# Moving the sample's score steps of the gated-linear-attention layer from the end of a block into the stretches of the next one

## The chip, the cores and the metric

The kernel runs on one core of one Trainium2 chip. The metric is the time of one execution on the device in microseconds (us). The engines in the profile are TensorE (PE, with its weight loads apart as PEld), VectorE (DVE), ScalarE (ACT), GpSimd (POOL) and SyncE (SP, here the issuer of most DMAs).

## The reference

One inference step of a decoder with two layers runs on a prompt of 2048 positions and on a sample group of 8 sequences with 4 new tokens each, 32 rows. The first layer is gated linear attention with 4 heads (128 key and 512 value elements each). Cut to what matters:

```
proj = rmsnorm(h) @ w_in                       # q, k, v, gate, g_low
log_a = log_sigmoid(g_low @ w_gate2 + b_gate) / 16
# in chunks, for each head:
b = cumsum(log_a)
rel = where(causal, b[t] - b[s], -inf)
scores = einsum('td,sd,tsd->ts', q, k, exp(rel))
out = (q * exp(b)) @ state + scores @ v
state = exp(b_last) * state + (k * exp(b_last - b)).T @ v
# then
o = rmsnorm(out) * silu(gate); h = h + o @ w_out
```

The prompt starts from a zero state; each of the 8 sequences starts from a state of its own (`state_gla`, 128 x 512 for each sequence and head), which is read, used and written back. The second layer is windowed attention on keys and values that are projected once; the change does not touch it.

## The kernel before

**Tiles.** The first layer works head by head, h = 0 to 3, and for each head in 4 blocks of 512 positions, (h, j), each of 4 chunks of 128. A product of two f32 operands is made of three matmuls on f16 halves (`PASSES`): an operand is split by ScalarE (L194 or L197, the high half) and VectorE (L195 or L198, the low half). Of each block the q and k projections (`qk_steps`, evicted by ScalarE at L430 into qT and kT), the decay (`decay_steps`, L366 to L372) and the prompt's scores (`level_steps`: a diagonal and 7 levels of halving spans, tiles E and X, PSUM bank lev) are prepared one block ahead. For each chunk, `vg_steps` projects V (split into v at L197/L198) and the gate (ScalarE at L477, VectorE at L478, tile sg), and `chunk_steps` makes the readout o and the state update kv. All projections use the PSUM tag pj with two banks; lev and kv have one bank each.

**The sample.** After the last block of a head, `SampleA` projects the 32 rows and returns 14 steps (L690 to L820): `diag`, two `level` steps, `mid`, `stack`, eight times `seq` and `fin`. `diag` computes the decay of the 32 rows and the diagonal of their scores S; a `level` makes an exponential (L721 to L725), splits it into the tile ssm (L194/L195), multiplies it on TensorE into lev, and writes the result into S under a mask (L731). `mid` makes the f16 copy Sh of S and the masked queries; `stack` transposes keys and values; `seq` reads one sequence's state (loaded for two sequences at a time, L785), splits it into pst (L197/L198), multiplies, updates it (L795, L796) and stores the pair (L800). The state tiles come from a ring (tag W) in which the third pair takes the buffer of the first. `fin` is at L806 to L814.

**The order.** The program is written as steps; `weave` puts a list of steps evenly between the steps of another, `mix` merges two lists. A block starts with `weave(cur.vg_steps(0, ...), prev_tail)`, where `prev_tail` is what the block before left over: its last chunk and the decay of the next block. Then come the q and k projections of the next block, and three stretches c = 0, 1, 2, in each of which V and gate of chunk c + 1 are woven with chunk c, some of the next block's levels, a share of the sample's steps (`sparts`), and preparations of weights for the second layer (L197/L198 from wraw, L248). In the first block of a head (j = 0, h > 0) the gate of chunk 0 comes after the q and k projections. The framework's scheduler then orders each engine's instructions by priorities that follow this text and by when it takes operands to be ready; the order on TensorE is fixed by the text only in the second layer. Each engine works through its instructions in order.

The last head's sample has no next block, and all its steps go into `prev_tail`. So the steps stand in three places where there is a next block: (1,0), (2,0) and (3,0).

Of the kernel before, what the change touches and what calls it, by code (L numbers as in the profile page):

```python
# [9 lines left out]
F32 = mybir.dt.float32  # L10
# [21 lines left out]
SMP = NS * TS  # L32
# [42 lines left out]
def _body(tc, nc, cp, sb, ps, dr, i, o):  # L75
    uniq = [0]

    def nm(s):
        uniq[0] += 1
        return f"{s}_{uniq[0]}"  # L80

    def T(tag, shape, dt, bufs=None):
        return sb.tile(shape, dt, tag=tag, name=nm(tag), **({} if bufs is None else {"bufs": bufs}))
# [67 lines left out]
    def weave(main, fill):  # L151

        main, fill = list(main), list(fill)
        done = 0
        for n, f in enumerate(main):
            f()
            upto = len(fill) * (n + 1) // len(main)
            for g in fill[done:upto]:
                g()
            done = upto  # L160
        for g in fill[done:]:
            g()
# [5 lines left out]
    def mix(a, b):  # L168

        out = []  # L170
        weave([lambda f=f: out.append(f) for f in a], [lambda f=f: out.append(f) for f in b])
        return out
# [125 lines left out]
    def norm_T(xh, n, dst, both=False, flat=False):  # L298
# [4 lines left out]
        if both:  # L303
            junk = T("S", [P, 512], F32, 1)
            dve.tensor_tensor_reduce(junk, xh[1], xh[1], 1.0, 0.0, ALU.mult, ALU.add, ss[:, 1:2])
# [110 lines left out]
    class Blk:  # L416
# [67 lines left out]
        def level_steps(self):  # L484


            def diag():
                S = self.S = T("S", [P, 512], F32, 1)
                Sv = S.rearrange("p (c t) -> p c t", t=P)
                E = T("E", [P, 512], F32, 2)  # L490
# [9 lines left out]
            def level(li, m):  # L500
                bt, S, qT, kT = self.bt, self.S, self.q, self.k
                NB = 256 // m
# [19 lines left out]
                for c in range(4):  # L522
# [8 lines left out]
                dve.copy_predicated(  # L531
                    S.rearrange("p (B z m) -> p B z m", z=2, m=m)[:, :, 1, :],
                    lvm[:, li, :].rearrange("p (B m) -> p B m", m=m),
# [135 lines left out]
    class SampleA:  # L669
# [18 lines left out]
        def steps(self):  # L688
# [4 lines left out]
            bx = {}  # L693
# [5 lines left out]
            def diag():  # L699
                if h == 0:  # L700
                    ogTs[0] = T("ogTs", [P, 16, 2, SMP], F16, 1)
                bx["bt"] = T("sbt", [P, SMP], F32, 1)
                logs(gls, h, SMP, rms, bx["bt"])
                qs, ks = self.qkv[:, 0, :], self.qkv[:, 1, :]
                S = bx["S"] = T("S", [96, SMP], F32, 1)
                X0 = dup3(T("ssm", [P, 2, 3, SMP], F16, 1), ks)
                X1 = dup3(T("sq2", [P, 2, 3, SMP], F16, 1), qs)
                pd = PT("lev", [P, 512])
                for n, (a, b) in enumerate(PASSES):
                    mm(pd[:96, :SMP], f(X0, a), X1[:, b, 0, :], start=n == 0, stop=n == 2)  # L710
                dve.tensor_tensor(S, pd[:96, :SMP], id3, ALU.mult)
# [194 lines left out]
    cur = Blk(0, 0, hw[0])  # L906
# [31 lines left out]
    prev_tail = []  # L938
    samp = None
    sparts = []  # L940

    for n, (h, j) in enumerate(blocks):
        nxt = None
        if n + 1 < len(blocks):
            h2, j2 = blocks[n + 1]
            nxt = Blk(h2, j2, hw[h2])
        side = []
        if n == 0:
            side = u_steps(2)
        elif n == 1:  # L950
            side = u_steps(3) + [us_step]
        lv = nxt.level_steps() if nxt else []
        last = j == NBL - 1
        late = j == 0 and h > 0
        if n > 0:
            weave(cur.vg_steps(0, (0,) if late else (0, 1)), prev_tail)
        if last:
            samp = SampleA(h, cur.w)
            for f in samp.proj_steps():
                f()  # L960
        if nxt:
            for f in nxt.qk_steps():
                f()
        if late:
            weave(cur.vg_steps(0, (1,)), [])
        if last:
            ch = [cur.chunk_steps(c) for c in range(3)]
            weave([f for c in range(1, 4) for f in cur.vg_steps(c, (0,))], ch[0] + lv[:3] + ch[1][:3] + lv[3:5] + ch[2][:3])
            run(hw[h + 1].v.steps() if h + 1 < AH else wo.steps()[4:])
            for c in range(1, 4):  # L970
                weave(cur.vg_steps(c, (1,)), (ch[c - 1][3:] if c > 1 else []) + lv[3 + c * 2 : 5 + c * 2])
            for f in ch[2][3:]:
                f()
            run(hw[h + 1].g.steps() if h + 1 < AH else wo1.steps()[8:])
        else:
            for c in range(3):
                if n == len(blocks) - 2:
                    if c == 0:
                        wo_aside()
                    more = (wo1.steps()[:8] + wo.steps()[:4])[c * 4 : c * 4 + 4]  # L980
                else:
                    more = side[c * 2 : c * 2 + 2] if n < 2 else some(PR[j])
                weave(cur.vg_steps(c + 1, (0, 1) if n else (1,)), mix(cur.chunk_steps(c) + lv[(0,3,6)[c]:(3,6,8)[c]], sparts[(0,3,7)[c]:(3,7,99)[c]]) + more)
                if j == NBL - 2 and h + 1 < AH and c == 0:
                    hw[h + 1] = head_weights(h + 1)
                    for u in hw[h + 1].qk:
                        for f in u.steps():
                            f()
            sparts = []
        if n == 0:  # L990
            gain(gs_o, i["a_out_norm"][0], later)
            gain(gs_kv, i["kv_norm"], later)
            gain(gs_b, i["b_norm"][0], later)

            def bf_const(name, shape):
                f = T("pst", shape, F32, 2)
                later(f, i["c_" + name])
                t = C(name, shape, BF16)
                dve.tensor_copy(t, f)
                return t  # L1000

            madd = bf_const("madd", [P, 2, P])
            nsink = C("nsink", [P, NKV * GRP], F32)
            later(nsink, i["b_sinks"][0].partition_broadcast(P))
            dve.tensor_scalar(nsink, nsink, -1.0, None, ALU.mult)
            gq = C("gq", [P, 2, HD], F32)
            for x_, g in enumerate((i["b_q_norm"][0], i["k_norm"])):
                later(gq[:, x_, :], g.partition_broadcast(P))

            lvs = C("lvs", [96, 2, 16], U8)  # L1010
            f_ = T("pst", [96, 2, 16], F32, 2)
            later(f_, i["c_lvs"])
            dve.tensor_copy(lvs, f_)
            id3 = C("id3", [96, SMP], F32)
            later(id3, i["c_id3"])
            bm = C("bm", [96, NS], F32)
            later(bm, i["c_bm"])
            bmq = T("spp", [P, NS, SMP], F16, 1)
            bmf = T("pst", [P, NS, SMP], F32, 2)
            later(bmf, i["c_bmq"])  # L1020
            dve.tensor_copy(bmq, bmf)
            smask = bf_const("smask", [P, 2, 160])
            rts = C("rts", [SMP, 4, HD], F32)
            for y_ in range(2):
                for z_ in range(2):
                    x_ = 2 * y_ + z_
                    later(rts[:, x_, :], i["c_rope_s"][z_])
                    if z_ == 0:
                        dve.tensor_tensor(rts[:, x_, :], rts[:, x_, :], gq[:SMP, y_, :], ALU.mult)
                    else:  # L1030
                        H2 = HD // 2
                        dve.tensor_tensor(rts[:, x_, :H2], rts[:, x_, :H2], gq[:SMP, y_, H2:], ALU.mult)
                        dve.tensor_tensor(rts[:, x_, H2:], rts[:, x_, H2:], gq[:SMP, y_, :H2], ALU.mult)
            sel = T("sq1", [GRP, P], F32, 1)
            later(sel, i["c_sel"])
            skT = C("skT", [GRP, NKV], F32)
            later(skT, i["b_sinks"][0].rearrange("(g r) -> r g", r=GRP))
            psk = PT("tr", [P, NKV], bufs=2)
            nc.tensor.matmul(psk, sel, skT, start=True, stop=True)
            sinkr = C("sinkr", [P, NKV], F32)  # L1040
            dve.tensor_scalar(sinkr, psk, 8.0, None, ALU.mult)
        prev_tail = cur.chunk_steps(3) + (nxt.decay_steps() if nxt else [])
        if j == NBL - 1:
            sparts = samp.steps()
            prev_tail += sparts[:4]
            del sparts[:4]
            if nxt is None:
                prev_tail += sparts
        cur = nxt
# [631 lines left out]
    for t in range(-3, NKV * NCH):  # L1681
        fill = []
        n = t + 3
        if n < NKV * NCH:
            g, c = divmod(n, NCH)
# [55 lines left out]
    for p_ in range(NCH // 2):  # L1741
        more = []
        if p_ + 1 < NCH // 2:
            nxt = pairs[p_ + 1]
            ld, sm = [lambda x=x, nxt=nxt: nxt.load(x) for x in (2, 3, 0, 1)], nxt.sums()
            more = ld[:2] + sm[:2] + ld[2:3] + sm[2:6]
# [3 lines left out]
        if p_ in (3, 4):  # L1750
            n = p_ - 3
# [88 lines left out]
```

## Time and profile before

| | |
|---|---|
| runs | 2853.12, 2844.96, 2841.90 us (median 2844.96) |
| profiled execution | 2844.21 us, span 2842.2 us, mean clock 0.987 |
| TensorE busy | 2723.1 us (96%) |
| VectorE busy | 1843.3 us (65%) |
| ScalarE busy | 1441.8 us (51%) |
| GpSimd busy | 1066.3 us (38%) |
| block (1,0), (2,0), (3,0): starts at about | 359, 632, 907 us |

A row of a timeline gives the start and length in us, the engine, the line, the operation, its output and inputs, their shapes, how many in a row (x), and in brackets the idle time before with what ended it. A row of the waits gives the engine and the tile that waited, the instruction that ended the wait, the sum in us, the number of waits and the longest. A row of the windows gives the stretch, its length, an engine's busy time, and the clock that TensorE was granted (1.00 is full speed).

### The profile page before, as it was taken

To read this page: it belongs to the slowest core of one execution; us is meant where nothing else is said; L and a number is where in the kernel's file an instruction comes from. 1 tells how busy PE (TensorE), PEld (TensorE's weight loads), DVE (VectorE), ACT (ScalarE), POOL (GpSimd) and SP (SyncE) were. 2 spreads that over 40 slices of the span, in tenths; PEclk is the share of its full clock that TensorE was granted. 3 is DMA by queue.
4 is the path that set the end of the run, shared out by engine and by line. 5 is a ranking of instruction groups with operands and counts; after the bars stand their busy time and mean duration, and the time that the engine had idled before them with its cause. 6 is when DMAs were issued, how large, how long until landed. Compare 5 with 4: busy or idle time off the path is not lost.

```text
span 2842.2 us, 51647 instructions
## 1 busy us (share of the span) xinstructions
PE 2723.1 (96%) x19070; PEld 1389.7 (49%) x19070; DVE 1843.3 (65%) x3815; ACT 1441.8 (51%) x3385; POOL 1066.3 (38%) x1471
## 2 busy tenths in 40 slices
PE   6899999999999999999899999999999999988999
PEld 4444444444454444445344555555555555553444
DVE  5767787668767785435512665677767767777653
ACT  6655666466546654433312555566666666651110
POOL 1242223222322221115504686666657657530000
PEclk9999999999999999999999999999999999999999
DMA  8351325123412442799977677957866788797651
GB/s 211 90 126 36 101 89 163 34 86 123 131 38 82 149 111 74 183 229 293 240 169 182 117 145 129 217 116 131 178 124 130 145 164 175 150 216 168 138 120 57
DMA packets 795606, 395.04 MB, mean 139 GB/s; under 512 B 647504, under 2 KB 721176, under 8 KB 795320
## 3 DMA queue, kind: packets, MB, share of 16 engines
q1 hardware_dynamic: 782392, 356.01, 55.4%
q0 software_dynamic: 10880, 35.66, 3.4%
q8 instruction: 149, 2.44, 0.4%
q14 instruction: 105, 0.86, 0.1%
q10 hardware_dynamic: 2080, 0.07, 0.0%
HBM read 144.28 MB, written 107.54 MB: 89 GB/s over the span
## 4 chain that ended last, share of the span: by engine, by line
PE 59%; DVE 12%; DMA 9%; ACT 8%; issue 6%; POOL 4%; SPq 1%; ACTq 0%; DVEq 0%; POOLq 0%
PE pj L101 34%; PE o L101 11%; PE tr L101 9%; PE kv L101 3%; ACT o L1278 2%; PE lev L101 2%; DVE v L198 2%; DMA pre<-pst 2%; ACT v L197 1%; DVE o L1273 1%; DMA wraw<-in_a_w_in_dram 1%; DVE W L198 1%; POOL ogT L195 1%; DVE lev L1273 1%; DVE X L195 1%
## 5 line engine op out<-in xcount | busy, mean ns | idle before, releaser
L101 PE MATMUL pj<-W,uT 128*128 128x512 f16 x5088 | 1199.7, 381 | 6.9 <-ACT qT L430 3.1
L101 PEld LDWEIGHTS <-uT 128*128 128x128 f16 x6976 | 653.3, 98 | 712.7 <-issue 35.2
L101 PE MATMUL tr<-W,uT 128*128 128x512 f16 x1536 | 365.5, 379 | 0.0
L186 POOL TENSOR_SCALAR rs_m<-ss 128x1 f32<-128x1 f32 (+3 forms) x190 | 46.0, 242 | 671.0 <-ACT og L611 230.8
L101 PEld LDWEIGHTS <-X 128*128 128x128 f16 x2744 | 184.5, 98 | 143.8 <-issue 11.7
L1278 ACT ACTIVATE o<-o,mx 128x256 f32<-128x256 f32 (+1 forms) x384 | 168.6, 439 | 163.7 <-DVE mx L1273 159.6
L101 PE MATMUL pj<-uT,W 128*128 128x512 f16 (+1 forms) x912 | 187.4, 356 | 27.6 <-DMA uT<-ogT 23.4
L1273 DVE CUSTOM_DVE_ANT_0 o<-o,madd,nsink 128x256 f32<-128x256 f32 (+1 forms) x384 | 183.9, 479 | 41.8 <-PE o L101 37.2
L187 POOL TENSOR_TENSOR rs_r<-rs_m,mhalf 128x1 f32<-128x1 f32 (+2 forms) x186 | 186.2, 1001 | 14.4
L198 DVE SCALAR_TENSOR_TENSOR v<-o,v 128x512 f16<-128x512 f32 (+1 forms) x192 | 128.8, 671 | 92.6 <-ACT v L197 90.4
L101 PEld LDWEIGHTS <-W 128*128 128x128 f16 x2448 | 129.8, 99 | 113.9 <-issue 19.7
L101 PEld LDWEIGHTS <-v 128*128 128x128 f16 x976 | 95.8, 98 | 126.7 <-issue 9.8
L508 POOL TENSOR_TENSOR E<-bt 128x256 f32<-128x256 f32 x96 | 74.2, 774 | 198.4 <-DVE X L195 118.0
L195 POOL TENSOR_TENSOR ogT<-og,ogT 128x512 f16<-128x512 f32 x68 | 87.9, 1293 | 154.8 <-ACT ogT L194 150.4
L101 PEld LDWEIGHTS <-sg 128*128 128x128 f16 x800 | 78.6, 99 | 102.6 <-DMA sg<-ogd 7.2
L101 PE MATMUL o<-gl,X 128*128 128x256 f16 (+1 forms) x768 | 113.7, 271 | 5.2 <-DMA X<-qe 2.8
L101 PE MATMUL pj<-W,v 128*128 128x512 f16 x448 | 107.0, 386 | 9.5 <-DVE st L1614 5.9
L197 ACT ACTIVATE v<-o 128x512 f16<-128x512 f32 (+1 forms) x192 | 111.2, 579 | 3.6
L1278 ACT ACTIVATE lev<-lev,mx 128x256 f32<-128x256 f32 (+1 forms) x128 | 56.5, 441 | 103.8 <-DVE mx L1273 101.8
L248 POOL DMA_DIRECT2D pre<-pst x72 | 50.5, 703 | 141.3 <-DVE pst L198 130.0
L195 DVE TENSOR_TENSOR X<-E,X 128x512 f16<-128x512 f32 x128 | 94.6, 739 | 12.8 <-ACT X L194 12.4
L194 ACT ACTIVATE X<-E 128x512 f16<-128x512 f32 x128 | 79.5, 621 | 43.4 <-PE lev L101 20.0
(468 smaller groups left out, 5021.4 us busy)
## 6 DMA issues: line engine op xcount, KB each, us to landing
pre<-pst POOLq DMA_DIRECT2D x72, 256.0 KB, 3.5
W<-pre SPq DMA_DIRECT2D x36, 512.0 KB
ogd<-ogT SPq DMA_DIRECT2D x68, 256.0 KB
wraw<-in_a_w_in_dram SPq DMA_DIRECT2D x64, 256.0 KB
wraw<-in_b_w_in_dram SPq DMA_DIRECT2D x64, 256.0 KB
oge<-ogT SPq DMA_DIRECT2D x64, 256.0 KB
wraw<-in_a_w_out_dram SPq DMA_DIRECT2D x32, 256.0 KB
X<-in_x_prompt_dram SPq DMA_DIRECT2D x32, 256.0 KB
```

The lines of the kernel that those rows point to most:

```text
L101: return order(nc.tensor.matmul(*a, **k))
L186: pool.tensor_scalar(m[:n, :k], ss, a, b, ALU.mult, ALU.add)
L187: pool.tensor_tensor(r[:n, :k], m[:n, :k], mhalf[:n, :k], ALU.pow)
L194: act(hi, src, AF.Copy)
L195: eng.tensor_tensor(lo, src, hi, ALU.subtract)
L197: act(hi, src, AF.Copy, scale=sc)
L198: dve.scalar_tensor_tensor(lo, src, sc, hi, ALU.mult, ALU.subtract)
L248: nc.gpsimd.dma_start(self.pre[:, :, half * 512 : half * 512 + 512], t)
L508: pool.tensor_tensor(Ev[:, :, 0, :], ref, btv[:, :, 0, :], ALU.subtract)
L1273: dve.tensor_tensor_reduce(pm[:, z], pm[:, z], madd.rearrange("p a b -> p (a b)")[:, (2 - nk) * P :], -0.125, nsink[:, g * GRP + h : g * G ...
L1278: act(pm[:, z], pm[:, z], AF.Exp, scale=-1.0, bias=nm_[:, h : h + 1], accum_out=bx["sum"][:, h : h + 1])
```

## The change

Three edits. The sample's score tile gets a tag of its own (sS) in place of the prompt's (S). At the end of a head's last block only `diag` goes into the tail that runs at the next block's start; before, the two levels and `mid` went there too. The remaining 13 steps are shared over the three stretches as 4, 5 and 4 (levels, `mid`, `stack`; sequences 0 to 4; sequences 5 to 7 and `fin`) where the remaining 10 were shared as 3, 4 and 3 (`stack` and sequences 0 and 1; 2 to 5; 6, 7 and `fin`).

```diff
-                S = bx["S"] = T("S", [96, SMP], F32, 1)
+                S = bx["S"] = T("sS", [96, SMP], F32, 1)
...
-                weave(cur.vg_steps(c + 1, (0, 1) if n else (1,)), mix(cur.chunk_steps(c) + lv[(0,3,6)[c]:(3,6,8)[c]], sparts[(0,3,7)[c]:(3,7,99)[c]]) + more)
+                weave(cur.vg_steps(c + 1, (0, 1) if n else (1,)), mix(cur.chunk_steps(c) + lv[(0,3,6)[c]:(3,6,8)[c]], sparts[(0,4,9)[c]:(4,9,99)[c]]) + more)
...
             sparts = samp.steps()
-            prev_tail += sparts[:4]
-            del sparts[:4]
+            prev_tail += sparts[:1]
+            del sparts[:1]
```

TensorE at the start of block (2,0), where the next block's k projection ends (its input W_5723) and the gate projection of chunk 0 begins (W_6862); before:

```order
L101 MATMUL pj_7079<-uT_157,W_5723 128x512
L101 LDWEIGHTS uT_156
L101 MATMUL pj_7106<-W_6862,uT_156 128x512 [waits Activation_49]
L101 LDWEIGHTS uT_156
L101 MATMUL pj_7106<-W_6862,uT_156 128x512
L101 LDWEIGHTS ssm_7000 [waits Activation_49]
L101 MATMUL lev_7003<-ssm_7000 96x16 [waits DVE_49]
```

The sample's first level stands between the second and the third matmul of the gate. With the change it stands behind the whole gate projection of chunk 0 and 16 matmuls of V of chunk 1 (into pj_7090), which itself has a wait on ScalarE (`...` for rows that repeat):

```order
L101 MATMUL pj_7062<-W_6889,uT_156 128x512
L101 LDWEIGHTS uT_156
L101 MATMUL pj_7090<-W_6638,uT_156 128x512 [waits Activation_49]
...
L101 MATMUL pj_7090<-W_6656,uT_156 128x512
L101 LDWEIGHTS ssm_7123
L101 MATMUL lev_7126<-ssm_7123 96x16 [waits DVE_49]
```

ScalarE at the same place, from the decay of the block (E, L366 to L368) and the levels' exponentials (L723) to the eviction of q (qT); before:

```order
L366 ACTIVATE E_7061<-tr_7059,bgate 128x512 [waits DVE_49,Activation_49]
L723 ACT_TABLE_LOAD
L723 ACTIVATE k_1190_6994<-k_1190_6994 128x32 [waits DVE_49]
L367 ACTIVATE E_7061<-E_7061 128x512 [waits Activation_49]
L723 ACTIVATE k_1194_7011<-k_1194_7011 128x32 [waits DVE_49]
L430 ACTIVATE qT_7077<-pj_7041 128x512 [waits PE_49]
```

And with the change, where qT stands ahead of L367 and of the second level's exponential, and the table load has gone to an earlier place:

```order
L366 ACTIVATE E_7017<-tr_7015,bgate 128x512 [waits DVE_49,Activation_49]
L723 ACTIVATE k_1205_7117<-k_1205_7117 128x32 [waits DVE_49]
L430 ACTIVATE qT_7033<-pj_6997 128x512 [waits PE_49]
L367 ACTIVATE E_7017<-E_7017 128x512 [waits Activation_49]
L723 ACTIVATE k_1214_7153<-k_1214_7153 128x32 [waits DVE_49]
```

SyncE in block (1,0), where the first head's pairs of states are stored (L800) and the next are loaded (L785), among stores of finished chunks (ogd) and a load for the second layer (L894); before:

```order
L623 DMA ogd_97<-ogT_4188 256x1x512 [waits DMAHW4_49,Pool_49]
L894 DMA pst_4309<-in_c_rope_dram 128x512 [waits DMAHW5_49,DMASW5_49,PE_49]
L800 DMA out_st_s_dram<-W_4221 128x2x512 [waits DMAHW6_49,DVE_49]
L785 DMA W_4433<-in_state_gla_dram 128x2x512 [waits DMAHW7_49,DMAHW6_49]
L623 DMA ogd_98<-ogT_4398 256x1x512 [waits DMAHW0_49,Pool_49]
```

And with the change, where the store of the first pair stands behind one more store of a chunk:

```order
L623 DMA ogd_97<-ogT_4155 256x1x512 [waits DMAHW5_49,Pool_49]
L623 DMA ogd_98<-ogT_4366 256x1x512 [waits DMAHW6_49,Pool_49]
L800 DMA out_st_s_dram<-W_4313 128x2x512 [waits DMAHW7_49,DVE_49]
L785 DMA W_4491<-in_state_gla_dram 128x2x512 [waits DMAHW7_49,DMAHW0_49]
L894 DMA pst_4508<-in_c_rope_dram 128x512 [waits DMAHW1_49,DMASW4_49,PE_49]
```

On all engines together the instructions are the same in kind, but for one more row on TensorE and two fewer on SyncE. After the last block of the first layer the orders do not differ.

## The prediction

> **What bounds the kernel now.** I read the page's table of engines first, to see which engine fills the span.
>
> ```profile
> PE 2723.1 (96%) x19070; PEld 1389.7 (49%) x19070; DVE 1843.3 (65%) x3815; ACT 1441.8 (51%) x3385; POOL 1066.3 (38%) x1471
> ```
>
> TensorE is busy 96% of 2842.2 us, and the change removes no instruction of any size from it. So what can be won is TensorE's idle time and its slow time at the three places where the sample's first four steps stand: the starts of the blocks (1,0), (2,0) and (3,0), which I call heads 1, 2 and 3. Next I read TensorE's waits there, with one window for each head (us in total, times, longest).
>
> ```profile
> PE lev L101 <- ACT ssm L194: 3.7, 1, 3.7
> ...
> PE lev L101 <- ACT ssm L194: 1.6, 1, 1.6
> PE pj L101 <- ACT qT L430: 1.5, 1, 1.5
> ...
> PE lev L101 <- ACT ssm L194: 1.6, 1, 1.6
> PE pj L101 <- ACT qT L430: 1.0, 1, 1.0
> ```
>
> The sample's level score (L101, into lev) waits for ScalarE's split of its operand, 3.7 us in head 1 and 1.6 us in heads 2 and 3; there the gate projection has also waited 1.5 and 1.0 us for the prompt's query eviction. Then the granted clock around these gaps (stretch, us, TensorE's busy us, clock, DMA share, GB/s).
>
> ```profile
> 355.20:358.90 3.70, 0.02 (x1) 1.00 0.01 2
> 359.20:362.60 3.40, 3.40 (x12) 0.55 0.00 0
> 632.70:639.40 6.70, 5.65 (x16) 0.50 0.00 0
> 909.10:912.50 3.40, 3.24 (x11) 0.50 0.02 5
> 445.00:455.00 10.00, 7.63 (x49) 1.00 0.57 189
> ```
>
> After each of the three gaps the clock is at about half for 3.4 us, in head 2 for 6.7; a stretch with 2.4 us idle elsewhere (the last row) keeps 1.00. What this cost is read from TensorE's timeline, here head 1 and then head 2.
>
> ```profile
> 358.88 0.21 PE L101 MATMUL lev<-ssm 128*96 128x16 f16 x1 [3.71 <-ACT ssm L194]
> 359.24 4.87 PE L101 MATMUL pj<-W,uT 128*128 128x512 f16 x14
> ...
> 624.52 5.56 PE L101 MATMUL pj<-uT,W 128*128 128x512 f16 x25
> 631.55 0.59 PE L101 MATMUL pj<-W,uT 128*128 128x512 f16 x2 [1.47 <-ACT qT L430]
> 633.75 0.25 PE L101 MATMUL lev<-ssm 128*96 128x16 f16 x1 [1.62 <-ACT ssm L194]
> 633.86 1.44 PE L101 MATMUL pj<-W,uT 128*128 128x512 f16 x3
> 635.24 4.00 PE L101 MATMUL pj<-W,uT 128*128 128x512 f16 x9
> 642.18 5.12 PE L101 MATMUL pj<-W,uT 128*128 128x512 f16 x23
> 647.91 2.32 PE L101 MATMUL pj<-W,uT 128*128 128x512 f16 x10
> ```
>
> At full clock a matmul of 512 columns takes 0.216 us: (5.56 - 0.38) / 24, where 0.38 is the one that ends a run. By that price the 14 of head 1 (4.87) lost 1.7 us to the clock, and the runs of 9 and 3 in head 2 (4.00 and 1.44) lost 1.9 and 0.6. Head 3 has the runs 2.96 and 1.44 in their place:
>
> ```profile
> 909.36 1.44 PE L101 MATMUL pj<-W,uT 128*128 128x512 f16 x3
> 910.75 2.96 PE L101 MATMUL pj<-W,uT 128*128 128x512 f16 x9
> 922.21 2.11 PE L101 MATMUL pj<-W,uT 128*128 128x512 f16 x9
> ```
>
> which lost 0.85 and 0.63. All that the three heads lose is thus about 3.7 + (1.47 + 1.62 + 2.5) + (0.96 + 1.61 + 1.5) + 1.7 = 15.1 us, half a per cent of the span.
>
> **What the change takes away, and what stands behind it.** The two levels and the middle step leave the block's start. In the order, the gate projection of chunk 0 (14 matmuls, then 10 mixed with 6 of the chunk before, 30 in all) now follows the key projection at once, then V of chunk 1, then the sample's first level. So the waits for ssm go. What TensorE meets next are two PSUM banks of the projections: V of chunk 1 needs the bank that ScalarE's eviction of kT empties, and the gate of chunk 1 the bank that VectorE's sg (L478) empties. The rows of head 2, ScalarE and then VectorE:
>
> ```profile
> 630.92 0.58 ACT L430 ACTIVATE qT<-pj 128x512 f32<-128x512 f32 x1
> 633.44 0.27 ACT L194 ACTIVATE ssm<-k 128x96 f16<-128x96 f32 x1
> 637.38 0.58 ACT L430 ACTIVATE kT<-pj 128x512 f32<-128x512 f32 x1
> ...
> 638.94 0.18 DVE L731 COPY_PREDICATED S<-lvs,lev 96x16 f32<-96x16 uint8 x1
> 639.02 0.25 DVE L195 TENSOR_TENSOR ssm<-k,ssm 128x96 f16<-128x96 f32 x1
> 645.55 0.68 DVE L478 SCALAR_TENSOR_TENSOR sg<-sg,pj 128x512 f32<-128x512 f32 x1
> ```
>
> *Head 1.* Here the eviction of qT ends at 358.08 + 0.58 = 358.66 (row below), and the ssm split 0.2 us later. The gate projection can begin at 358.66 in place of 358.88, and one key matmul that stood behind the level (0.2) runs inside the gap: 0.4 us won. A gap of 3.3 us is left, and from the rows above (1.47 and 1.62 us with half a microsecond of work between halve the clock) I take it that the 1.7 us of half clock stay; if they went, the end would be 1.7 us earlier, inside the forecast's own range.
>
> ```profile
> 358.08 0.58 ACT L430 ACTIVATE qT<-pj 128x512 f32<-128x512 f32 x1
> ```
>
> [...]
>
> *Head 2.* The key projection ends at 624.52 + 5.56 = 630.1. ScalarE's order moves qT ahead of one exponential of the decay, so I take qT to be done by then. The 30 matmuls run at full clock, 30 x 0.216 = 6.5 us, to 636.6. V of chunk 1 waits for kT: ScalarE's work in front of it is the same in kind, so its end stays at about 637.4 + 0.58 = 637.96, a new wait of 1.4 us. V's 24 matmuls (5.2) reach 643.2. The gate of chunk 1 then waits for sg. From kT's end VectorE works without a pause through to L478, whose end was 645.55 + 0.68 = 646.23. Of the rows in between, one level's L731 and L195 leave (0.18 + 0.25), so sg ends at 645.8, a new wait of 2.6. Before, that projection began after the last 4 of V's matmuls in the run at 647.91, so at 648.8. It begins 3.0 us earlier; small matmuls and transposes that stood ahead of it now stand behind (I count 0.7), so 2.3 us are won of 5.6 lost. The two new gaps, 1.4 and 2.6 us, lie apart with 5.2 us of full work between, like the 2.4 us gap that kept its clock.
>
> *Head 3* in the same way: sg ended at 922.0 and now at 921.6; the gate of chunk 1 began at 922.21 + 4 x 0.216 = 923.1. That is 1.5 us earlier, less the 0.7: 0.8 us.
>
> ```profile
> 921.34 0.68 DVE L478 SCALAR_TENSOR_TENSOR sg<-sg,pj 128x512 f32<-128x512 f32 x1
> ```
>
> **What it adds.** The levels cost TensorE 6 matmuls of 16 columns wherever they stand (0.1 to 0.3 us a row, unchanged). The score tile of its own costs 32 elements a partition and no instruction; it frees the prompt's score tile, which nothing on the chain above waits for. The blocks (1,1), (2,1) and (3,1) change their order too and have waits of their own, all on evictions (one row of head 1's):
>
> ```profile
> PE kv L101 <- DVE v L198: 2.4, 1, 2.4
> ```
>
> I price them at nothing, bounded by this row from both sides: a stall of such a size may come or go in one of the three, plus or minus 3 us.
>
> The later steps are squeezed: the middle step, the stack and the eight sequences stand in less room. Between the last matmul of a pair of sequences and the first of the pair that reuses its state tile, the order has 43 matmuls for the pair 0-1, or 43 x 0.216 = 9.3 us at bare rate and about 10 with the small ones and transposes among them. In this time VectorE updates the state, SyncE stores it, loads the next, and ScalarE splits it:
>
> ```profile
> 384.04 0.68 DVE L796 SCALAR_TENSOR_TENSOR W<-kv,W 128x512 f32<-128x512 f32 x1
> 384.75 0.41 SPq L800 DMA_DIRECT2D out_st_s_dram<-W  x1
> 387.94 0.38 SPq L785 DMA_DIRECT2D W<-in_state_gla_dram  x1
> 392.14 0.63 ACT L197 ACTIVATE pst<-W 128x512 f16<-128x512 f32 x1 [1.18 <-DMA W<-in_state_gla_dram]
> ...
> 400.29 0.38 SPq L800 DMA_DIRECT2D out_st_s_dram<-W  x1
> 406.94 1.15 ACT L197 ACTIVATE pst<-W 128x512 f16<-128x512 f32 x2 [0.93 <-DMA W<-in_state_gla_dram]
> ```
>
> From the update's start to the end of the split that is 392.14 + 0.63 - 384.04 = 8.7 us, and the second store takes 6.7 from issue to use where the first takes 7.4. With 10 us of cover, about 1 us of margin is left: cost nothing, if the loads do not grow.
>
> **The sum** against the profiled execution (2844.2, of which 2842.2 span; the median of the runs shown is 0.8 above it): 0.4 + 2.3 + 0.8 = 3.5, so 2844.2 - 3.5 = 2840.7, rounded to **2841 us**. The forecast is a gain too small to be told from none: what a measurement here can tell from no change is about 0.5%, 14 us.
>
> **The rivals.** *All of the stalls go* (B): the clock stays up in every head but the first, and no new bank wait takes the place of the old. For it: kT and sg may come sooner, since the eviction of kT stands behind a chain on ScalarE that the level's split lengthened. Against it: from kT to sg VectorE has no gap to give up. It gives 0.4 + 5.6 + 4.1 = 10.1 us: 2834.
>
> *Nothing moves* (D): the steps that are taken from the head come back as VectorE and ScalarE work ahead of kT or sg in the following stretch, and the gate of chunk 1 begins when it did. The wait only changes its name: 2844. For it: these two engines, not TensorE, are what the three heads wait for in every row above.
>
> *The squeezed sequences run late* (C), the other side: a pair's state comes after TensorE wants it. Its place is the first matmul of the sequences 4 and 6 in (1,1) to (3,1), 2 pairs in 3 heads. Each microsecond of the chain of store, load and split beyond its cover costs 6. The gain of 3.5 is used up at 0.6 us beyond the margin, that is when the chain takes 8.7 + 1 + 0.6 = 10.3 us. At 2 us beyond the margin it costs 12: 2844.2 - 3.5 + 12 = 2853. For it: the split waits for the load already (1.18 and 0.93 us of ScalarE's time above), and the store stands in SyncE's queue behind others. Against it: the chain has to grow by a fifth.
>
> **How the numbers follow.** The forecast 0.50, D 0.20, C 0.17, B 0.13. Eight in ten lie from B with 2 us below it to most of C: 2832 to 2851; the plus or minus 3 us of the later blocks lies within. The forecast's own range, with its 3 us on both sides, is 2838 to 2844. Faster by over 0.5% needs below 2831, a little beyond B: 0.05. Slower by over 0.5% needs above 2859, C at 3 us beyond the margin: 0.05. Within: 0.90.
>
> **What will show it.** In the profile of the changed kernel the waits of lev on ssm near 355, 632 and 908 us are gone. In their place, in heads 2 and 3, projections wait for ACT kT (about 1.4 us) and for DVE sg L478 (about 2.6), and the stretches of clock 0.50 there read 1.00; head 1 keeps a gap of 3.3 us, named after qT, and half clock behind it. A wait of o on pst, or a long ScalarE wait for the load of the state, would be C. If head 1 reads 1.00 after its gap, my reading of the clock fails there. The prediction as a whole is wrong if the blocks after the heads gain or lose more than 3 us each, of which nothing in the old trace could tell.

## The result

The changed kernel takes 2872.36 us (median of 6 runs, 2860.42 to 2879.73), the kernel before 2843.43 (6 runs). The ratio is 1.0081 with a 95% interval of 1.0063 to 1.0099: 0.8% slower, about 23 us (the two medians lie 29 us apart), where a gain of 3.5 us was forecast and the range ended at 2851. The profiled execution of the changed kernel has a span of 2870.2 us, 28 us longer.

### The profile after

First the table of engines of the changed kernel, then TensorE's waits in the three heads, one window for each (us in total, times, longest).

```profile
PE 2737.9 (95%) x19070; PEld 1392.3 (49%) x19070; DVE 1846.1 (64%) x3815; ACT 1440.0 (50%) x3385; POOL 1073.0 (37%) x1471
...
PE pj L101 <- ACT qT L430: 2.5, 1, 2.5
PE pj L101 <- DVE sg L478: 0.5, 1, 0.5
PE lev L101 <- DVE ssm L195: 0.3, 1, 0.3
...
PE pj L101 <- DVE sg L478: 2.7, 1, 2.7
PE pj L101 <- ACT kT L430: 1.2, 1, 1.2
...
PE pj L101 <- DVE sg L478: 2.6, 1, 2.6
PE pj L101 <- ACT kT L430: 1.2, 1, 1.2
```

The waits for ScalarE's half of ssm, 3.7, 1.6 and 1.6 us, are gone (0.3 us for VectorE's half is left in head 1), and in heads 2 and 3 the waits for kT and sg have come in their place, 1.2 and 2.7 us where 1.4 and 2.6 were forecast. So these waits came as the prediction says, and the loss is elsewhere. Where, a table of six stretches shows: for each head the block (h,0) from the start of the q and k projections that stand in it to those in (h,1), and (h,1) from there to those in (h,2) (stretch, length, TensorE's busy time, clock, DMA share, GB/s). Before:

```profile
343.57:425.21 81.64, 77.27 (x451) 0.98 0.31 95
425.21:494.29 69.08, 64.05 (x375) 1.00 0.55 172
619.08:700.59 81.51, 78.43 (x451) 0.96 0.27 89
700.59:770.72 70.13, 64.68 (x374) 1.00 0.53 164
895.10:975.34 80.24, 77.32 (x451) 0.98 0.28 91
975.34:1042.97 67.63, 64.19 (x374) 1.00 0.60 171
sum 450.23, PE 425.94; mean PE 70.99
```

The same six of the changed kernel:

```profile
344.85:428.75 83.90, 78.06 (x452) 0.98 0.26 80
428.75:500.57 71.82, 67.33 (x373) 0.95 0.54 166
625.13:709.92 84.79, 78.58 (x452) 0.98 0.23 77
709.92:784.45 74.53, 67.49 (x373) 0.95 0.54 164
908.70:993.03 84.33, 78.46 (x453) 0.98 0.23 75
993.03:1065.85 72.82, 65.39 (x373) 0.98 0.59 168
sum 472.19, PE 435.31; mean PE 72.55
```

The six blocks are 472.2 - 450.2 = 22.0 us longer: 9.6 us in the three blocks (h,0), and 12.3 us in the three blocks (h,1), in which no step of the sample stands in the text. The other blocks of the first layer between (1,0) and (3,2) keep their length within 0.4 us. Outside the six, this execution is another 6 us longer; a second execution of the same order (shared_tile below) is 3.1 us longer there, and nothing is built on it.

By these tables (length less busy time) TensorE's idle time rose from 10.4 to 17.9 us in (h,0) and from 13.9 to 19.0 in (h,1). The half clock (granted 0.50), priced at half of the time that it lasted (the most that it can have cost), went from 6.8 to 5.1 us in (h,0) and from nothing to 8.5 in (h,1).

In (h,1) TensorE waits for what ScalarE and VectorE make, in the three blocks 18.9 us where it was 12.0; for the split of V alone 13.1 where it was 9.5. Of block (2,1), the kernel before and then the changed one:

```profile
PE kv L101 <- ACT v L197: 2.4, 2, 1.7
...
PE kv L101 <- DVE v L198: 4.1, 2, 2.2
PE kv L101 <- ACT v L197: 1.5, 2, 0.9
```

In (h,0) the new waits stand near the end. ScalarE's and TensorE's waits there, of the first head:

```profile
ACT pst L197 <- DMA W<-in_state_gla_dram: 9.1, 2, 6.2
...
PE o L101 <- ACT pst L197: 1.8, 1, 1.8
PE o L101 <- DVE pst L198: 0.7, 2, 0.4
```

Before, ScalarE's first line read 2.1 us in two waits, and TensorE had neither of the others in this head. The rows of the changed kernel behind it, VectorE, SyncE, ScalarE and TensorE:

```profile
401.65 0.68 DVE L796 SCALAR_TENSOR_TENSOR W<-kv,W 128x512 f32<-128x512 f32 x1
...
403.76 0.56 SPq L800 DMA_DIRECT2D out_st_s_dram<-W  x1
408.50 0.37 SPq L785 DMA_DIRECT2D W<-in_state_gla_dram  x1
...
412.30 1.15 ACT L197 ACTIVATE pst<-W 128x512 f16<-128x512 f32 x2 [6.22 <-DMA W<-in_state_gla_dram]
...
412.98 0.38 PE L101 MATMUL o<-pst,qe 128*128 128x512 f16 x1 [1.81 <-ACT pst L197]
```

From the store's issue to the split 8.5 us pass (7.4 and 6.7 before), and ScalarE stands still for 6.2 of them; TensorE waits 1.8. In heads 2 and 3 ScalarE stands for 5.0 and 5.6 us at this place. In the kernel before it stood there too, for 0.9, 1.4 and 1.6 us.

### The profile page after: what moved, and what is told of

The parts are those of the page before. It is cut to its first block, busy times and chain, and to the rows that moved or that the text cites. A ratio compares the mean times of both kernels' runs of the same rounds, so it can differ in the third digit from the quotient of the medians.

```text
span 2870.2 us, 51645 instructions
## 1 busy us (share of the span) xinstructions
PE 2737.9 (95%) x19070; PEld 1392.3 (49%) x19070; DVE 1846.1 (64%) x3815; ACT 1440.0 (50%) x3385; POOL 1073.0 (37%) x1471
## 4 chain that ended last, share of the span: by engine, by line
PE 48%; DVE 15%; DMA 12%; ACT 10%; issue 8%; POOL 6%; SPq 1%; ACTq 0%; POOLq 0%; DVEq 0%
PE pj L101 28%; PE tr L101 8%; PE o L101 8%; PE kv L101 2%; ACT o L1278 2%; DVE v L198 2%; DMA pre<-pst 2%; ACT v L197 1%; PE lev L101 1%; DVE o L1273 1%; DMA wraw<-in_a_w_in_dram 1%; POOL ogT L195 1%; DVE X L195 1%; DMA W<-in_state_gla_dram 1%; DVE pst L198 1%
```

## The experiments

Each edit is to the kernel before or to the changed kernel, as said. "(h,0)" and "(h,1)" are the lengths of the three blocks together, against the kernel before, from one profiled execution each; the ratio is of the times, with its interval, to runs of the kernel before that were made along with it.

| run | edit to | ratio to before | (h,0) us | (h,1) us |
|---|---|---|---|---|
| the change | | 1.0081 [1.0063, 1.0099] | +9.6 | +12.3 |
| shared_tile | changed | 1.0080 [1.0061, 1.0099] | +11.5 | +7.8 |
| seq_early | changed | 1.0043 [1.0026, 1.0059] | +5.1 | +8.0 |
| seq_late | before | 1.0057 [1.0039, 1.0075] | +6.8 | +7.5 |
| levels_gate | before | 1.0064 [1.0050, 1.0078] | +8.7 | +3.5 |
| no_levels | changed | 1.0052 [1.0033, 1.0071] | +1.6 | +11.0 |
| after_pr | changed | 1.0073 [1.0055, 1.0091] | +7.0 | +4.9 |
| before_pr | before | 1.0057 [1.0043, 1.0071] | -3.4 | +5.3 |
| cut48 | before | 1.0057 [1.0035, 1.0079] | +1.5 | +7.4 |
| mid_only | before | 0.9997 [0.9984, 1.0011] | -2.1 | -0.4 |
| after_pr0 | changed | 1.0057 [1.0035, 1.0079] | +2.8 | +9.8 |
| before_pr0 | before | 1.0039 [1.0020, 1.0057] | -1.2 | +9.7 |
| after_noload | changed | 1.0049 [1.0032, 1.0067] | +0.2 | +9.4 |
| before_noload | before | 1.0031 [1.0019, 1.0044] | -3.2 | +5.9 |
| after_pr2 | changed | 1.0059 [1.0042, 1.0075] | +9.7 | +9.0 |
| before_pr2 | before | 1.0031 [1.0015, 1.0047] | +2.0 | +6.9 |
| after_lg | changed | 1.0071 [1.0047, 1.0095] | +10.3 | +6.6 |
| after_noload_lg | changed | 1.0029 [1.0015, 1.0043] | +2.0 | +3.3 |
| before_lg | before | 1.0017 [1.0001, 1.0033] | -0.7 | +4.6 |

The order of shared_tile is that of the changed kernel, so the two rows show how far two profiled executions of one order differ: 2 us in (h,0), 4.5 in (h,1).

### One edit at a time: the sequences, the levels, the tile

seq_early:

```diff
-sparts[(0,4,9)[c]:(4,9,99)[c]]
+sparts[(0,6,10)[c]:(6,10,99)[c]]
```

> The change with one edit altered: the 13 steps are shared as 6, 4 and 3 (levels, middle step, stack and sequences 0 and 1; sequences 2 to 5; 6, 7 and the last step), so that the sequences stand in the same stretches as before the change and only the levels and the middle step have moved. Theory 1 (the sequences are late): the 22 us that the changed kernel loses in the six blocks (1,0) to (3,1) come from the sequences that moved back by a stretch; with them in their old stretches the waits of o on pst go and the blocks (1,1), (2,1) and (3,1) are as long as before the change, so 2838 to 2847 us. Theory 2 (the levels in the stretches): the levels' chain over ScalarE, VectorE and the bank of lev disturbs the prompt's own scores wherever it is mixed in, so 2858 to 2872 us here too, and (1,1) to (3,1) stay 3 to 5 us longer each.

seq_late (with the score tile's own tag, which moves nothing in the order by itself):

```diff
-sparts[(0,3,7)[c]:(3,7,99)[c]]
+sparts[(0,1,6)[c]:(1,6,99)[c]]
```

> The kernel before with the levels and the middle step left in the tail, as they were, and only the sequences moved back: the 10 remaining steps are shared as 1, 5 and 4 (stack; sequences 0 to 4; 5 to 7 and the last step). Theory 1 (the sequences are late): it loses like the changed kernel, most of 22 us, so 2855 to 2872 us, with (1,1) to (3,1) 3 to 5 us longer each. Theory 2 (the levels in the stretches): about the time of before, 2840 to 2850 us.

shared_tile:

```diff
-S = bx["S"] = T("sS", [96, SMP], F32, 1)
+S = bx["S"] = T("S", [96, SMP], F32, 1)
```

> The changed kernel without its first edit: the sample's score tile shares the prompt's buffer again, while the steps stand where the change puts them. The order of all engines is that of the changed kernel. If the tile of its own does something, the prompt's scores and the sample's now wait for each other and this is slower than the changed kernel by several us in each of (1,0), (2,0), (3,0), over 2880 us. If it does nothing, as both theories say, the time is the changed kernel's, 2860 to 2880 us.

The tile does nothing: 1.0081 with it and 1.0080 without. Neither theory holds alone. The sequences back by a stretch cost 0.6% with the head untouched, and the head's steps in the stretch cost 0.4% with the sequences in their place. Both lengthen (h,1) by about the same, though they move different steps.

### The levels beside the gate, no levels, and the preparations shared otherwise

levels_gate (with the score tile's own tag too):

```diff
-            weave(cur.vg_steps(0, (1,)), [])
+            weave(cur.vg_steps(0, (1,)), sparts[:3])
+            del sparts[:3]
...
-            prev_tail += sparts[:4]
-            del sparts[:4]
+            prev_tail += sparts[:1]
+            del sparts[:1]
```

> The kernel before with the two levels and the middle step moved only a little: they are woven with the gate projection of chunk 0, which follows the q and k projections, and all later steps stand where they stood before the change (10 steps shared as 3, 4 and 3). In the order on TensorE the first level now follows 12 matmuls of the gate, in place of none or 2. If the loss of the changed kernel comes from what the moved steps add to the stretches, this keeps the good of the move without it: the waits for ssm (3.7, 1.6 and 1.6 us) and the half clock behind them in the second and third head (3.4 and 1.7 us) go, the waits for qT stay, and (1,1) to (3,1) are as long as before: 2834 to 2842 us. If the wait is only passed on to kT and sg, as in the changed kernel: 2842 to 2846 us. If any move of these steps lengthens the blocks (1,1) to (3,1): over 2850 us.

no_levels:

```diff
-return [diag, lambda: level(0, 2), lambda: level(1, 1), mid, stack] + ...
+return [diag, lambda: None, lambda: None, mid, stack] + ...
```

> The changed kernel without the two level steps of the sample in all four heads (their exponentials, splits, 6 matmuls and masked writes), so the sample's scores keep only their diagonal. If the levels' own chain in the stretches makes the loss, this takes most of it away: 2840 to 2850 us. If the later place of the sequences and of the middle step makes it, most stays: 2855 to 2868 us.

after_pr, and before_pr as its control:

```diff
-PR = (1, 4, 2, 0)
+PR = (1, 2, 4, 0)
```

> The changed kernel with fewer preparations of the second layer's weights in the blocks (h,1): 2 in place of 4 for a stretch, and 4 in place of 2 in (h,2); the number over a head is the same. If the blocks (1,1) to (3,1) lose because work that spills over from (h,0) meets the many preparations there on VectorE and ScalarE, they shrink by 3 to 5 us each and the time is 2850 to 2860 us. If the preparations have no part in it: 2862 to 2880 us.

> The kernel before with the same other share of preparations (2 for a stretch in (h,1), 4 in (h,2)), as the control of the run on the changed kernel. If the preparations only hurt together with the work that spilled over: 2838 to 2848 us. If they hurt by themselves, this is faster than before by as much as the changed kernel gains from it.

levels_gate was to be the better version, and is slower than before. The waits for ScalarE's ssm are gone and new ones stand behind; the state comes late in its third head as well, though the sequences stand where they did in the text:

```profile
PE lev L101 <- DVE sS L731: 1.9, 2, 1.4
PE o L101 <- ACT pst L197: 1.6, 1, 1.6
```

Without the levels, the loss in (h,0) nearly goes (+1.6 of +9.6) and that in (h,1) stays (+11.0): the two are different losses. TensorE's waits for pst stay too, 5.5 us in the three blocks (h,0). With the preparations shared otherwise, the two kernels are equally long in (h,1) (+4.9 and +5.3), but before_pr loses by itself, also in (h,2) and (h,3) (8 us), so the preparations' number in (h,1) is no proof.

### Earlier sequences, the middle step alone, more room in (h,0)

cut48, in the kernel before:

```diff
-sparts[(0,3,7)[c]:(3,7,99)[c]]
+sparts[(0,4,8)[c]:(4,8,99)[c]]
```

> The kernel before with only the sharing of the 10 later steps altered, and in the direction that makes the sequences earlier: 4, 4 and 2 in place of 3, 4 and 3. Head, levels and middle step stay in the tail. If what costs is work that comes late and spills over the border into (h,1), this is not slower than before: 2836 to 2846 us. If any reordering of the sequences among the stretches makes (h,1) longer than it is in the kernel before, whose order happens to fit, it loses too: 2852 to 2862 us, most of it in (1,1), (2,1) and (3,1).

mid_only, in the kernel before:

```diff
-            prev_tail += sparts[:4]
-            del sparts[:4]
+            prev_tail += sparts[:3]
+            del sparts[:3]
...
-sparts[(0,3,7)[c]:(3,7,99)[c]]
+sparts[(0,4,8)[c]:(4,8,99)[c]]
```

> The kernel before with only the middle step moved from the tail into the first stretch (4, 4 and 3 steps in the stretches); the levels stay in the tail, the sequences where they stood. If the work added to the first stretch counts by its amount, this adds one step of three and loses about a third of what the run with all three moved lost (14 us): 2845 to 2850 us. If any reordering costs about the same: 2852 to 2862 us.

after_pr0 and before_pr0:

```diff
-PR = (1, 4, 2, 0)
+PR = (0, 4, 3, 0)
```

> The changed kernel with no preparations of the second layer's weights in the stretches of (h,0), in place of 1 each, and 3 in place of 2 in those of (h,2); (h,1) keeps its 4. If the loss is a backlog of ScalarE and VectorE that the three added steps build up in (h,0) and carry into (h,1), the room made here takes it away: the decay of the next block (VectorE L372) comes at 3 us after the start of the q and k projections in place of 5 to 9, (2,1) and (3,1) shrink by 3 to 5 us each, and the time is 2850 to 2860 us. If not: 2862 to 2880 us.

> The control of the run on the changed kernel: the kernel before with the same sharing of preparations (0, 4 and 3 for a stretch). If the kernel before has no backlog in (h,0): no gain, 2840 to 2848 us, or a loss if the preparations cost more where they now stand. If room in (h,0) is worth something to it too: under 2838 us.

These split the question. Sequences that come earlier lose as well (cut48, +7.4 in (h,1)), so lateness is not what (h,1) pays for. mid_only moves a step and loses nothing. Laying the profiled rows of ScalarE and VectorE of its three blocks (h,1) beside those of the kernel before, 1 of 209 and 0 of 246 stand in another place; in the changed kernel it is 95 and 97. In each of the other runs at least 5 rows of every block had moved, and all of them lose 3.3 us or more there. The (h,1) blocks of mid_only have the length of before (71.82, 74.53 and 72.82 in the changed kernel):

```profile
423.59:493.50 69.91, 65.66 (x374) 0.98 0.55 170
...
699.71:768.50 68.79, 64.56 (x375) 1.00 0.54 168
...
972.72:1040.51 67.79, 65.36 (x375) 0.97 0.60 171
```

More room in (h,0) made (h,0) shorter (+2.8) and left (h,1) (+9.8); its control loses as much in (h,1) with the head untouched.

### No late loads, and more preparations in (h,0)

after_noload and before_noload:

```diff
-if b % 2 == 0:
-    bx["sr"] = T("W", [P, 2, 512], F32, NW)
+if b % 2 == 0 and b < 4:
+    bx["sr"] = bx[b] = T("W", [P, 2, 512], F32, NW)
     nc.sync.dma_start(bx["sr"], ...)
+elif b % 2 == 0:
+    bx["sr"] = bx[b - 4]
```

> The changed kernel in which sequences 4 to 7 of heads 0 to 2 read no state of their own but go on in the tiles of sequences 0 to 3 (their two loads for each head are left out, all stores stay), so ScalarE cannot wait for a late load. If ScalarE's waits in front of the loads (3 and 5 to 6 us in each head) are what holds its queue and pushes the preparations into (h,1): the waits of o on pst in (h,0) go, 5 or more preparations are done before (h,1) begins, (1,1) to (3,1) are as long as in the kernel before, and the time is 2842 to 2852 us. If only TensorE's own waits for pst and the half clock behind them go (5 and 2 us), with (h,1) still long: 2858 to 2868 us.

> The control: the kernel before without the same loads. Its ScalarE waits for them too, 1 to 3 us at a time, but TensorE did not: 2838 to 2848 us, not told from the kernel before. If the loads' waits cost it too: under 2835 us.

after_pr2 and before_pr2:

```diff
-PR = (1, 4, 2, 0)
+PR = (2, 4, 1, 0)
```

> The changed kernel with 2 preparations for a stretch in (h,0) in place of 1, and 1 in place of 2 in (h,2). If the preparations that slide out of (h,0) are the cause of the loss in (h,1), listing them earlier brings 5 or 6 of them back ahead of (h,1), and (2,1) and (3,1) shrink by 3 us or more each: 2855 to 2865 us. If (h,0) has no room for them, they slide out again and nothing is won: 2862 to 2880 us.

> The control, and the mirror of the run with none listed in (h,0): the kernel before with 2, 4 and 1 preparations for a stretch. If a preparation more ahead of (h,1) is worth 2 us, as the run with fewer suggests: (2,1) and (3,1) shrink by 2 us each and the time is 2834 to 2842 us. If the kernel before already has as many there as fit: 2840 to 2850 us.

Without the late loads, the changed kernel's three blocks (h,0) have the length of before: 243.6 us together, against 253.0 with the loads and 243.4 before. Its rows of them follow. In the first, TensorE's waits are 1.9 us for qT, 0.5 for sg and 0.3 for ssm; none for pst is left.

```profile
345.36:424.17 78.81, 76.10 (x453) 1.00 0.25 77
...
619.19:701.69 82.50, 78.11 (x454) 0.98 0.22 75
...
900.50:982.76 82.26, 78.21 (x454) 0.98 0.22 74
```

So the loss in (h,0) goes with the late state. The control gains 3.2 us there, so without the late loads 6 to 9 of the 9.6 us go. Without the levels 8.0 of the same 9.6 went, though the state was still late; so the two shares can't be added, and how the levels and the late state divide the loss is not shown. (h,1) keeps +9.4: the theory that ScalarE's stand in front of the load pushes the preparations into (h,1) and so makes it longer falls. The preparations' place falls too: in before_noload, 6 to 8 preparations were done ahead of (h,1), where the kernel before had 5 or 6, and (h,1) was still 5.9 us longer; after_pr2 won nothing there that two executions of one order don't differ by.

### The decay ahead of the gate

In the changed kernel ScalarE evicts a chunk's gate (L477) ahead of the next block's decay (L368), and the second of its two table loads stands at L510, in the chain of the prompt's scores, and no longer at L477. Of the kernel before, then of the changed one, block (2,1):

```profile
699.14 1.28 ACT L368 ACT_TABLE_LOAD   x1
...
702.45 1.28 ACT L477 ACT_TABLE_LOAD   x1
703.75 0.60 ACT L477 ACTIVATE sg<-pj 128x512 f32<-128x512 f32 x1
```

```profile
712.36 0.57 ACT L477 ACTIVATE sg<-pj 128x512 f32<-128x512 f32 x1
...
714.19 1.28 ACT L368 ACT_TABLE_LOAD   x1
...
729.14 1.28 ACT L510 ACT_TABLE_LOAD   x1
```

after_lg, before_lg, and after_noload_lg (with the edit of after_noload):

```diff
-logs(gl[:, self.j], self.h, 512, rmask, self.bt)
+with tc.high_priority(offset=100 if self.j == 2 and self.h > 0 else 0): logs(gl[:, self.j], self.h, 512, rmask, self.bt)
```

> The changed kernel with one priority altered: in the blocks (1,1), (2,1) and (3,1) the next block's decay is scheduled 100 places sooner, which puts it ahead of the gate's eviction on ScalarE again, as in the kernel before, and the table load back to L477. If the decay's place is the cause of the loss in (h,1): these three blocks shrink by 3 to 4 us each to about their length in the kernel before, while (h,0) stays 9 us too long, so 2850 to 2860 us. If it only goes along with the loss: 2862 to 2880 us.

> Both causes taken out of the changed kernel: the decay sooner, and sequences 4 to 7 without loads of their own (the two later loads of each of the heads 0 to 2 are left out). If late loads cost the 9 us in (h,0) and the decay's place the 12 us in (h,1), nothing of the loss is left: 2838 to 2848 us. If another cause is at work in (h,1): 2852 us or more, as without the earlier decay (2859).

> The control: the kernel before with the same priority. Its decay already stood ahead of the gate's eviction, so if only that place counts, 2840 to 2848 us. If what the sooner decay does beside it (kT and the splits of the scores come ahead of a weight preparation on ScalarE) is worth something by itself: 2830 to 2840 us.

The order came out as wanted; the table load is back at L477 in all three blocks. The time of after_lg did not move clear of noise: 1.0071 against 1.0081 and 1.0080, as expected if the place only goes along with the loss. Its (h,1) is 6.6 us too long, against 12.3 and 7.8 in the two executions of the changed order, and without the loads 3.3 against 9.4. The pair without the loads differs by 6.1 us there and by 0.2% in time, with intervals that overlap; so a part of the decay's place is neither shown nor excluded. With both edits the time is 2855.1 us, where nothing was to be left of the loss if the two were all of it (2838 to 2848). 1.0029 is left of 1.0081, about what the controls lose: 1.0031 for the loads alone, 1.0017 for the decay alone, in kernels whose head is untouched.

## Why the prediction was wrong

**The heads: the mechanism held, with the clock mis-sized.** The new waits are the forecast ones, but for head 1's gap, 2.5 us where 3.3 was forecast. TensorE's idle time on the waits of the heads was 9.4 us (3.7 + 1.5 + 1.6 + 1.0 + 1.6) and is 11.0 (the seven waits shown under the result). The forecast let the clock stay up behind the two new gaps of heads 2 and 3; it fell behind the second of them, and in head 1, where half clock was to stay, it did not fall (clock in the fourth column):

```profile
358.30:361.70 3.40, 3.37 (x16) 1.00 0.00 0
652.80:656.30 3.50, 3.50 (x11) 0.63 0.00 0
936.10:939.50 3.40, 3.40 (x11) 0.64 0.00 0
```

Both misses have the same root: the prediction took the size of a gap for what counts, and the rows of the last section show full clock behind gaps of 2.5 and 2.4 us and half clock behind gaps of 2.3 and 1.9. The clock's part fell from 6.8 us to 3.4 at the heads, so these gained about 6.8 - 3.4 - 1.6 = 1.8 us, not 3.5.

**The squeezed sequences: the step that failed first.** "With 10 us of cover, about 1 us of margin is left: cost nothing, if the loads do not grow." They grew. From the update at 401.65 to the end of the split, 412.93, the second reuse took 11.3 us where 8.7 was reckoned from the first: the store was issued 2.1 us after the update began (0.7 before), and the load 4.7 us after the store (3.2 before). TensorE waited 1.8, 0.6 and 1.2 us in the three heads, 5.3 us with VectorE's half of the split. So the rival C has its place and its mechanism right, and its size in head 1: 1.6 us beyond the cover of 9.7. It counted six such waits, and three came. With the 1.7 us of half clock behind the first of them (0.50 for 3.41 us from 414.83) this makes 7.0 us, of the 6 to 9 that (h,0) has less without the late loads. That ScalarE's stand costs more than this through what is queued behind it is not shown: in after_pr0 it stands for 4.3, 4.2 and 4.5 us at this place, and (h,0) is 2.8 us longer.

**The blocks (h,1): the larger step that failed.** "I price them at nothing, bounded by this row from both sides", 3 us in one of the three. They lost 12.3 us in the profiled execution and 7.8 in the other of the same order. What the runs show is that the loss goes with a changed order of ScalarE and VectorE there, whatever changed it: fewer or more preparations, earlier or later sequences, no loads, an earlier decay; and that it is absent in the one other run that keeps this order. Idle time and the price of half clock in these three blocks make 13.9 us in the kernel before, 14.3 in mid_only, and 17.4 to 27.5 in the kernels with another order. So the wait rows of the old trace bounded nothing: they show what this one order cost, and another order has other waits, with half clock behind them (five stretches of 3.41 us at 0.50 in the changed kernel, none before). That the order is the cause is argued from this going along, and which single displacement in it costs how much stays open. Of two candidates that were tried, the preparations' place was not borne out, and the decay's place is not decided.

**The chances** put 0.17 on C and 0.05 on a loss of over 0.5%. The cases were built from the places where the sample's steps stand, though the prediction itself says that the blocks (h,1) change their order, and in the profiles nearly half of ScalarE's rows and four in ten of VectorE's stand there in other places.

## What to carry to other kernels

When an order that a scheduler makes is changed at one place, count the rows that move on the other engines in the blocks behind it; a block whose TensorE waits are all on evictions can grow with no step of its own moved, and its present waits don't say by how much (here 3 to 12 us in three blocks). When a load reuses a buffer that must first be stored, reckon its chain with the store's wait in its queue and the load's wait behind the store: here 2.1 and 4.7 us, where 0.7 and 3.2 had been read from the old order. Before a move is called a loss or a gain, move each of its parts alone: here the middle step was free (ratio 0.9997), and the levels and the sequences were not.

## What the runs showed of the hardware

The size of a gap alone did not tell whether half clock stood behind it. In the kernel before, the six blocks have three stretches of half clock (0.50), of 3.4, 6.8 and 3.4 us, one in each head; behind the gap of 2.4 us in block (1,1) the clock stayed at 1.00. In the 3.4 us ahead of the half clock TensorE was busy for 0.72 us in head 1 and 1.42 in head 2. In head 2 it was busy for 2.32 of the first 3.41 us at half clock, and another 3.41 at half clock followed. Rows of the kernel before (stretch, length, busy, clock):

```profile
356.18:359.60 3.42, 0.72 (x6) 1.00 0.01 2
359.60:363.01 3.41, 3.41 (x10) 0.50 0.00 0
629.25:632.66 3.41, 1.42 (x6) 1.00 0.27 50
632.66:636.07 3.41, 2.32 (x9) 0.50 0.00 0
636.07:639.48 3.41, 3.41 (x10) 0.50 0.00 0
...
448.34:451.76 3.42, 1.48 (x7) 1.00 0.43 144
451.76:455.17 3.41, 3.41 (x28) 1.00 0.75 243
```

In the changed kernel the six blocks have eight stretches of half clock, of 3.41 us each. Behind head 1's gap of 2.5 us, which ends at 358.33, the clock stayed at 1.00; behind gaps of 2.3 and 1.9 us in block (1,1), which end at 455.75 and 471.84, it was 0.50:

```profile
356.80:360.22 3.42, 1.89 (x9) 1.00 0.01 2
360.22:363.63 3.41, 3.41 (x17) 1.00 0.00 0
452.38:455.79 3.41, 1.13 (x8) 1.00 0.19 70
455.79:459.20 3.41, 3.41 (x19) 0.50 0.76 237
469.44:472.86 3.42, 1.53 (x12) 0.99 0.78 220
472.86:476.27 3.41, 3.41 (x10) 0.50 0.61 201
```

The busy time of the stretch ahead does not part the cases cleanly either: 1.48 us were followed by full clock in the kernel before, and 1.53 by half clock in the changed one. What decides is not shown. Two gaps close together (1.47 and 1.62 us, head 2 of the kernel before) had 6.8 us of half clock behind them, one of 3.7 us (head 1) 3.4 us.
